# Order of copies, splits, loads and banks in the last third of a decoder layer kernel

## The chip, the cores and the metric

The kernel runs on one core of a Trainium2 chip. The core has a matmul engine (TensorE, PE in the profile; PEld is its weight load, which overlaps with it), a vector engine (VectorE, DVE), an activation engine (ScalarE, ACT), a general engine (GpSimd, POOL) and a queue engine (SyncE, SP) that here only issues transfers. Each runs its own list of instructions in order and waits on semaphores for the others. The metric is the device time of one execution in microseconds (us); the median of several runs counts.

## The reference

One layer on x of 512 tokens by 1024, in float32: three token mixers in parallel (a gated MLP over chunks, sparse attention, a recurrent block), merged through gates and an output projection, then a SwiGLU. Cut to what matters here:

```python
h = rms_norm(x, g_pre_mix)
z = h @ w_in
u, v, q, kv, nsa_g, xr, rg, mg = jnp.split(z, split_points, axis=-1)
...
merged = (gates[:, :, 0] * (y_a @ w_br_a)
          + gates[:, :, 1] * (y_b @ w_br_b)
          + gates[:, :, 2] * (y_c @ w_br_c))
x = x + rms_norm(merged @ w_o, g_post_mix)

hf = rms_norm(x, g_pre_ffn)
f_gate, f_up = jnp.split(hf @ w_ffn_in, 2, axis=-1)
f = (jax.nn.silu(f_gate) * f_up) @ w_ffn_out
return x + rms_norm(f, g_post_ffn)
```

`w_ffn_in` is 1024 by 5632 (gate and up of 2816 each), `w_ffn_out` 2816 by 1024.

## The kernel before

**Numbers.** A float32 operand goes to PE as two parts: `hi`, a copy on ACT rounded to the type that PE multiplies at full rate (line L131 in the profile), and `lo`, the rest, a subtraction on DVE (L136). `split` issues both. A product is then three matmuls: hi by hi, hi by lo, lo by hi.

**Block products.** Where it can, the kernel cuts a matrix product into 2x2 blocks and computes it with seven block products in place of eight, after the scheme of Strassen in Winograd's form: sums and differences of blocks are made on DVE ahead (`s13`, `a21`, `a22` for the weights; `tokens` for the other side), and the seven results are added in PSUM banks or on DVE.

**c stage.** In an earlier part, `b_pair` computes the branch projections with such products while `wload` prepares weight tiles for later; `wload` loads a tile on SP and splits it. `with tc.issue_after(x)` puts what it holds behind instruction x in the scheduler's list, so on each engine behind what stands there by then.

**Gate and up, `ffn_head` and `pairs`.** The 22 column pairs of `w_ffn_in` (a gate tile and the up tile beside it) are computed for two halves of the tokens. `ffn_head` does the first two pairs (`HEAD = 2`) with plain passes for the first half of tokens; `passes` runs over eight blocks k of the depth, from block `turn` on. `pairs` does the other 20 (j = 2 to 21). A pair is seven products `a11, s1, s2, a12, s4, s3, a22`, each of 12 matmuls of 128x256, 84 in all; PE runs them as a11, s1, (a22 of the pair before), s2, a12, s4, s3. The product z of s2 is copied to `r1` on ACT, that of s1 to `r3`, y (a12 and s4) is added to `r1` on DVE, silu follows on ACT; z of s3 is copied to `r2` on ACT, `r3` is added on DVE; after a22 of the pair, `r1 * r2` gives the slab `f`.

**Weights of a pair.** Its raw tile `rawp` holds two rows of tiles per partition, u = 0 (raw0: a11 and a12) and u = 1 (raw1: a21 and a22), 1 MB in all, in one of two alternating buffers (j = 5 has a third). `pair_prep(j)` is a generator in five steps: split raw0 and make `s13` from both halves; split `s13`; split a22 and make a21 in place; make a22 in place; split raw1 (now holding what products s2 and s4 need) and load pair j + 2 into the same buffer (`pair_load`). The split tiles come from a ring of five. `pairs` takes a step of the preparation of pair j + 1 between the products of pair j. What order results on each engine, the scheduler settles from the order of issue and the buffers. The lines are L1698 for the load, L1717 s13, L1726 a21, L1728 a22, L1740 the matmuls, L1768, L1771, L1781 and L1798 the copies of a11, s1, s2 and s3, L1792 the add to r1, L1793 silu, L1799 the add to r2, L1755 the product into f.

**Last projection, `down`.** Seven block products of four quarters q each, 12 matmuls of 128x512 a quarter, with plain `block`s for the part that the scheme leaves over. `fo["prep"]` makes the operands of a quarter: (b) the weights and (a) the tokens, each split by ACT and DVE; for some, `down_add` lets a transfer on POOL's queue add the next weight block into the raw tile after the split. `product(n, q)` runs over two depth blocks i and two PSUM banks m. At the end the last units' blocks are done for each of four token rows c, and `close` finishes row c (L1876 the matmuls of all this).

Of the kernel before, what the change touches and what calls it, by code (L numbers as in the profile page):

```python
# [27 lines left out]
AF = mybir.ActivationFunctionType  # L28
# [24 lines left out]
def hybrid_block(ctx: ExitStack, tc: tile.TileContext, A, out):  # L53
# [84 lines left out]
    res = {}  # L138
# [109 lines left out]
    def unit():  # L248
        i = wcur[0]
        wcur[0] += 1  # L250
        wload(i + 3)
        return wready.pop(i)
# [1064 lines left out]
    def c_stage(first):  # L1317

        c_raw(0)
        gelu = (*res["hid"], res["w1"])  # L1320
        sums = after(gelu, yc_sums())
        second = compress(1)

        def begin():
            for _ in range(4):
                next(sums)
                yield
                head = res["hi"]
            prep = after((head, res["sum"], *gelu), b_prep(0))
            for g in (prep, prep, first, prep, sums, sums, prep, prep, sums, sums, prep):  # L1330
                next(g)
                if g is first:
                    compress_w2(1)
                yield
            c_raw(1)
            c_raw(2)

        run([c_gate(2), hidden(second), c_gate(3)], begin(), 1.5)
        more = seq(second, gmlp_prep(), v_norm())

        def load():
            with tc.issue_after(res["out"].ins):
                wload(wlimit[0])

        for p in range(4):
            pair = b_pair(p, "c")
            third = res["s3"]
            prep = iter(())
            for i, _ in enumerate(pair, 1):
                if p < 3:  # L1350
                    if i == 3:
                        wlimit[0] += 1
                        load()
                    if i == 4:
                        prep = after((*third, res["out"]), b_prep(p + 1))
                    if p and i in (4, 5, 6, 7, 9):
                        next(prep)
                elif i == 2:
                    wlimit[0] = B0 + 4
                    with tc.issue_after(res["out"].ins):  # L1360
                        wload(C0 + 9)
                elif i == 5:
                    with tc.issue_after(res["out"].ins):
                        wload(C0 + 10)
                if i in ((), (1, 2, 3, 5, 7, 8), (), (1, 2, 3, 5, 7, 9))[p]:
                    next(more, None)
            if p == 0:
                wlimit[0] += 1
                load()
                next(prep)  # L1370
            for n, j in enumerate({0: (4, 5), 1: (6,), 2: (7,), 3: ()}[p]):
                if p == 0:
                    next(more)
                side = itertools.islice(more, 3 if p == 1 else 0) if p else itertools.islice(prep, 3 if n == 0 else 1)
                run([c_gate(j)], side, 1.0)
            for _ in prep:
                pass
            if p == 0:
                c_raw(3)
        for _ in more:  # L1380
            pass
# [197 lines left out]
    def ffn_head(n):  # L1579

        us, bs = [], []
        for i in range(2 * n):
            us.append(unit())
            bs.append(bank("mm"))
            yield from passes(bs[i], *us[i], res["fh"], res["fl"], n1=256, turn=0 if i else 4)
            yield

        z, y = ff["zy"] = bank("mm")[:, :256], bank("mm")
        yield from product_parts(z, n, "a11", 11)
        yield from product_parts(y[:, :256], n, "a12", 21)  # L1590

        for j in range(n):
            for k0 in range(0, NK, 4):
                for i in (2 * j, 2 * j + 1):
                    hi, lo = us[i]
                    for k in range(k0, k0 + 4):
                        for t, (w, x) in enumerate(((hi, res["fh"]), (hi, res["fl"]), (lo, res["fh"]))):
                            PE.matmul(bs[i][:, 256:], w[:, k * 128:k * 128 + 128], x[k][:, 256:], start=(k == t == 0),  # L1598
                                      stop=(k == NK - 1 and t == 2))
                        if k % 2:  # L1600
                            yield
            ffn_out(j, bs[2 * j], bs[2 * j + 1])
# [90 lines left out]
    def pair_raw(j):  # L1693
        return ff["raw"][2 if j == HEAD + 3 else (j - HEAD) % 2]

    def pair_load(j):
        if HEAD <= j < NFF:
            SY.dma_start(pair_raw(j), A["w_fi"][2 * j:2 * j + 2].rearrange("u p n -> p u n"))  # L1698

    def pair_prep(j):  # L1700

        if j >= NFF:
            return
        raw = pair_raw(j)
        r4 = raw.rearrange("p u (h n) -> p (u h) n", h=2)
        a11, a12, a21, a22 = (r4[:, i] for i in range(4))
        g = [ff["ring"][(3 * (j - HEAD) + i) % 5] for i in range(3)]
        w = wa[j] = {}

        def halves(u, *names):  # L1710
            for i, n in enumerate(names):
                w[n] = tuple(t[:, 512 * i:512 * i + 512] for t in u)

        split(raw[:, 0], *g[0])
        halves(g[0], "a11", "a12")
        s13 = stage.tile([128, 1024], F32, tag="raw", name=nm("s13"), bufs=2)
        V.tensor_tensor(s13.rearrange("p (i n) -> p i n", i=2), r4[:, 0:4:3], a21[:, None, :].to_broadcast([128, 2, 512]),  # L1717
                        op=OP.subtract)
        yield
        split(s13, *g[1])  # L1720
        halves(g[1], "s3", "s1")
        yield
        side = 32 * ((j - HEAD + 1) % 2)
        w["a22"] = row("a22h", F32R, "tg", side), row("a22l", F32R, "q32", side)
        split(a22, *w["a22"])
        V.tensor_add(a21, s13[:, 512:], a11)  # L1726
        yield
        V.tensor_sub(a22, a12, a21)  # L1728
        yield
        split(raw[:, 1], *g[2])  # L1730
        halves(g[2], "s2", "s4")
        if j != HEAD + 1:
            pair_load(j + 2)
        yield

    def product_parts(ps, j, a, b, start=True):
# [8 lines left out]
    def pairs():  # L1745
# [12 lines left out]
        for j in range(HEAD, NFF):  # L1758
# [31 lines left out]
            yield  # L1790
            product(y[:, 256:], j, "s4", 22, False)
            V.tensor_add(r1, y, r1)  # L1792
            res["silu"] = SC.activation(r1, r1, AF.Silu)  # L1793
            next(prep, None)
            yield
            r2 = row("r2")
            product(z, j, "s3", 3, False)
            SC.activation(r2[:, 256:], z, AF.Copy)  # L1798
            V.tensor_add(r2[:, 256:], r2[:, 256:], r3[:, :256])  # L1799
            wa[j].update(z=z, r1=r1, r2=r2)  # L1800
            next(prep, None)
            yield
        down_begin()
        wlimit[0] = len(wlist)
# [24 lines left out]
    def down_begin():  # L1829
        s1 = slab("fs1", tag="y", shape=(NQ, 2, 256))  # L1830
        for q in range(NQ):
            f = ff["slab", q]
            for i in range(2):
                for h in range(2):
                    fo[f"a{h + 1}{i + 1}", q] = f[:, i:4:2, 256 * h:256 * h + 256]
            fo["s1", q] = s1[:, q]
        fo["n"] = 0
        fo["a"] = {}

        def prep(n, q, hi, lo):  # L1840
            a, b, after = {1: ("a11", "c", (0, 1)), 2: ("a12", "b", None), 5: ("s1", "c", (1, 1)),
                           6: ("a11", "c", (1, 0)), 3: ("a12", "d", (0, 1)), 7: ("a21", "d", None),
                           4: ("a22", "c", None)}[n]
            e = (2, 3, 0, 1)[fo["n"] % 4]
            fo["n"] += 1
            split(fo[b, q], *(t.rearrange("p (i n) -> p i n", i=2) for t in (hi, lo)))
            if after:
                down_add(b, q, *after)
            u = ff["unit"][e // 2][:, e % 2].rearrange("p (l i t) -> p l i t", l=2, i=2)
            fo["a"][n, q] = u[:, 0], u[:, 1]  # L1850
            split(fo[a, q], u[:, 0], u[:, 1])
        fo["prep"] = prep

    def fo_sum(name, q):
# [8 lines left out]
    def down():  # L1863
# [24 lines left out]
        def product(n, q):  # L1888
            ps = {1: z, 6: z, 7: z, 4: z, 2: y, 5: w, 3: w}[n]
            bh, bl = unit()  # L1890
            ah, al = fo["a"].pop((n, q))
            for i in range(2):
                f = slice(512 * i, 512 * i + 512)
                for m in range(2):
                    t = slice(128 * m, 128 * m + 128)
                    mac(ps[m], (ah[:, i, t], bh[:, f]), (ah[:, i, t], bl[:, f]), (al[:, i, t], bh[:, f]))

        def plain(h, i):
# [78 lines left out]
        plain(1, NS + 2)  # L1977
        products(4, *((close, 1, c) for c in range(4)))
        us = [unit() for _ in range(NS, NP)]
        for c in range(4):  # L1980
            for i, u in enumerate(us):
                block(0, c, NS + i, *u)
            close(0, c)


# [217 lines left out]
```

## Time and profile before

| what | value |
|---|---|
| three runs | 1092.98, 1093.83, 1094.03 us, median 1093.83 |
| span of the profiled execution | 1090.5 us |
| the median over that span | 3.3 us more |
| DMA, mean over the span | 106 GB/s |
| split, lo of the gate/up halves and others (L136, lo<-raw) | 104 instructions, 1164 ns each |

The span runs from the first to the last instruction that the profiler saw; a time measured from outside has some us around it, and no other time of the profiled execution itself is on record. On the page the busy share of each engine stands first; the chain of waits names, from the end backwards, what each engine waited for; a timeline row shows start, length, engine, line, what it writes and reads, and in brackets the idle time ahead of it and what ended it. In the names, `mm` and `tr` are PSUM banks, `t` and `fh`, `fl` tokens, `hi`, `lo` and `u` split weights, `r` rows of the pair, `s` the tile s13.

### The profile page before, as it was taken

Reading aid. Unit: us, or ns where it says so; the run is one execution under the profiler, and the core shown is the slowest. Engines: PE = TensorE matmul, PEld = TensorE weight load, DVE = VectorE, ACT = ScalarE, POOL = GpSimd, SP = SyncE. Lnnn points to the kernel's source line nnn. Section 1 sums busy time; section 2 is a strip of 40 time slices with the busy share of each in tenths; the row PEclk is TensorE's granted clock in tenths of the full one; section 3 lists DMA queues with packets and bytes.
Section 4 is the critical chain, followed back from the end, with each engine's and each line's share of the span. In section 5 each row is a group of like instructions: output and inputs, shape, how many; then the busy total and the mean of one; then the engine's idle time right before and its main releaser. Section 6 shows DMA issues by size and latency. Waiting matters only on the chain.

```text
span 1090.5 us, 16726 instructions
## 1 busy us (share of the span) xinstructions
PE 1080.7 (99%) x6440; PEld 948.2 (87%) x6440; DVE 883.2 (81%) x1552; ACT 658.9 (60%) x1207; POOL 30.2 (3%) x43
## 2 busy tenths in 40 slices
PE   9999999999999999999999999999999999999997
PEld 7888888999889888898888789988999999998885
DVE  6967779669675899998998887877987888889665
ACT  6757574454444676876777655555656665667552
POOL 1000000000000000000000000000000000022200
PEclk9999999999999999999999999999999999999999
DMA  8332325420322211102111134261323232379902
GB/s 313 104 103 84 97 85 199 182 99 20 116 78 78 78 59 39 59 20 78 59 39 59 58 119 134 76 251 39 117 78 117 100 117 94 135 213 219 185 21 96
DMA packets 34943, 115.06 MB, mean 106 GB/s; under 512 B 3440, under 2 KB 3728, under 8 KB 33968
## 3 DMA queue, kind: packets, MB, share of 16 engines
q1 hardware_dynamic: 28064, 96.93, 26.0%
q0 software_dynamic: 5216, 11.18, 5.1%
q10 hardware_dynamic: 1584, 5.90, 1.4%
q8 instruction: 50, 0.82, 0.3%
q14 instruction: 29, 0.24, 0.1%
HBM read 111.89 MB, written 2.10 MB: 105 GB/s over the span
## 4 chain that ended last, share of the span: by engine, by line
PE 96%; DVE 2%; DMA 1%; ACT 1%; issue 0%; SPq 0%; DVEq 0%; ACTq 0%
PE mm L259 37%; PE mm L1740 16%; PE mm L1876 7%; PE mm L1260 7%; PE mm L1496 4%; PE o L979 4%; PE mm L614 4%; PE sc L941 3%; PE tr L966 3%; PE tr L1876 3%; PE mm L857 2%; PE tr L771 1%; PE tr L498 1%; PE mm L1598 1%; DMA raw<-in_w_v 1%; PE tr L674 1%
## 5 line engine op out<-in xcount | busy, mean ns | idle before, releaser
L259 PE MATMUL mm<-hh,hi 128*128 128x512 f32 x504 | 199.5, 396 | 0.0
L259 PE MATMUL mm<-hh,lo 128*128 128x512 f32 x504 | 197.4, 392 | 0.0
L259 PE MATMUL mm<-hl,hi 128*128 128x512 f32 x504 | 197.0, 391 | 0.0
L136 DVE TENSOR_TENSOR lo<-raw,hi 128x1024 fp32r<-128x1024 f32 (+1 forms) x104 | 121.1, 1164 | 36.9 <-ACT hi L131 34.0
L131 ACT ACTIVATE hi<-raw 128x1024 fp32r<-128x1024 f32 (+1 forms) x104 | 105.2, 1011 | 50.3 <-PE mm L259 18.9
L259 PEld LDWEIGHTS mm<-hh,lo 128*128 128x128 f32 x504 | 94.6, 188 | 19.6
L259 PEld LDWEIGHTS mm<-hl,hi 128*128 128x128 f32 x504 | 94.7, 188 | 18.4 <-issue 0.2
L259 PEld LDWEIGHTS mm<-hh,hi 128*128 128x128 f32 x504 | 94.7, 188 | 18.1 <-PE mm L1260 0.2
L947 ACT ACTIVATE P<-P,ast 128x128 f32<-128x128 f32 (+3 forms) x128 | 70.7, 555 | 23.0 <-DVE ast L945 22.2
L945 DVE CUSTOM_DVE_ANT_0 P<-sc,mask 128x128 f32<-128x128 f32 (+3 forms) x128 | 57.9, 484 | 8.1 <-PE sc L941 7.3
L131 ACT ACTIVATE ph<-tr 128x512 fp32r<-128x512 f32 x80 | 46.9, 592 | 26.2 <-PE tr L966 23.0
L136 DVE TENSOR_TENSOR pl<-tr,ph 128x512 fp32r<-128x512 f32 x80 | 54.4, 686 | 2.9 <-ACT ph L131 0.9
L941 PE MATMUL sc<-K,q 128*128 128x512 f32 (+2 forms) x192 | 51.0, 368 | 0.0
L1740 PE MATMUL mm<-t,hi 128*128 128x256 f32 x288 | 50.7, 276 | 0.0
L1876 PE MATMUL mm<-hi,u 128*128 128x512 f32 x160 | 50.4, 390 | 0.1
L966 PE MATMUL tr<-ident,P 128*128 128x128 f32 x320 | 48.7, 273 | 0.0
L966 PEld LDWEIGHTS tr<-ident,P 128*128 128x128 f32 x320 | 39.1, 140 | 9.6 <-DVE pl L136 1.0
L136 DVE TENSOR_TENSOR lo<-bs,hi 128x1024 fp32r<-128x1024 f32 x28 | 34.1, 1222 | 13.6 <-ACT hi L131 13.5
L1740 PEld LDWEIGHTS mm<-t,hi 128*128 128x128 f32 x288 | 43.3, 188 | 0.0
L1740 PE MATMUL mm<-fh,hi 128*128 128x256 f32 x144 | 40.0, 278 | 0.0
L1740 PE MATMUL mm<-fh,lo 128*128 128x256 f32 x144 | 39.8, 276 | 0.0
L1740 PE MATMUL mm<-fl,hi 128*128 128x256 f32 x144 | 39.8, 276 | 0.0
(474 smaller groups left out, 2895.0 us busy)
## 6 DMA issues: line engine op xcount, KB each, us to landing
raw<-in_w_in SPq DMA_DIRECT2D x64, 512.0 KB, 3.5
rawp<-in_w_fi SPq DMA_DIRECT2D x20, 1024.0 KB, 4.8
bs<-in_w_fo POOLq DMA_DIRECT2D x20, 512.0 KB, 7.4
raw<-in_w_br SPq DMA_DIRECT2D x14, 512.0 KB, 3.5
w<-in_cw ACTq DMA_DIRECT2D x4, 1024.0 KB, 7.3
raw<-in_w_o SPq DMA_DIRECT2D x8, 512.0 KB, 3.9
bs<-in_w_fo SPq DMA_DIRECT2D x8, 512.0 KB, 7.9
raw<-in_w_v SPq DMA_DIRECT2D x7, 512.0 KB, 5.1
```

The costliest lines, as they stand in the source:

```text
L131: res["hi"] = SC.activation(hi, src, AF.Copy)
L136: res["lo"] = V.tensor_sub(lo, src, f32(hi))
L259: res["mm"] = PE.matmul(ps[:m, n0:n1], w[:, k * 128:k * 128 + m], x[k][:, n0:n1], start=(t == 0), stop=(t == 3 * NK - 1))
L614: res["mm"] = PE.matmul(b[c], x[k][:, c * 128:(c + 1) * 128], w[:, kk * 512:kk * 512 + 512], start=(k == 0 and t == 0), stop=(k == NK - 1 ...
L941: PE.matmul(ps[:, :w * n].rearrange("p (b n) -> p b n", b=w), lhs, K[:, i, brs[0]:brs[-1] + 1, :n], start=(i == 0), stop=(i == 1))
L945: V.tensor_tensor_reduce(out=t, in0=ps[:, b * n:b * n + n], in1=mask[0][:, S - n:], scale=-0.125, scalar=3.0e38, op0=OP.add, op1=OP.min, a ...
L947: SC.activation(t, t, AF.Exp, scale=-1.0, bias=st[:, 0, j, b:b + 1], accum_out=st[:, 1, j, b:b + 1])
L966: PE.transpose(pt[:, j * 128:(j + 1) * 128], self.part(j, br)[:, kt * 128:(kt + 1) * 128], ident)
L979: PE.matmul(po, VV[:, kt, g % 2, br].rearrange("p i d -> p (i d)"), x, start=(br == 0 and kt == 0 and t == 0), stop=(br == 1 and kt == a a ...
L1260: res["mm"] = PE.matmul(ps, u[:, k * 128:k * 128 + 128], v[:, k], start=(start and k == t == 0), stop=(k == 3 and t == 2), skip_group_chec ...
L1740: res["mm"] = PE.matmul(ps, w[:, k * 128:k * 128 + 128], x[:, k], start=(start and k == t == 0), stop=(k == 3 and t == 2), skip_group_chec ...
L1876: PE.matmul(ps, a, b, start=id(ps) not in begun, stop=i == len(ops) - 1, skip_group_check=True)
```

## The change

It touches seven places, all of them orders; sums, products and shapes stay.

1. c stage: in the last `b_pair`, the weight tile `C0 + 9` is loaded and split one step later, behind the copy of another product.
2. `ffn_head`: the first unit runs over depth blocks 0 to 7, no longer 4 to 7 and then 0 to 3.
3. `pair_load` may load one half; in `pair_prep` half 0 of pair j + 2 is loaded after the a22 step, half 1 after the split of raw1. Twenty transfers of 1 MB become forty of 512 KB; the first two and the third buffer's go together still.
4. `pairs`: the copy of s3 is issued first, and silu and all the rest of the preparation behind that copy.
5. `down`, operands: tokens are split ahead of weights.
6. `down`, products: one PSUM bank after the other, no longer in turns.
7. The end: the blocks of the first leftover unit for c = 0 and 1 are issued ahead of all others.

```diff
-                elif i == 2:
+                elif i == 3:
                     wlimit[0] = B0 + 4
                     with tc.issue_after(res["out"].ins):
                         wload(C0 + 9)
...
-            yield from passes(bs[i], *us[i], res["fh"], res["fl"], n1=256, turn=0 if i else 4)
+            yield from passes(bs[i], *us[i], res["fh"], res["fl"], n1=256)
...
-    def pair_load(j):
+    def pair_load(j, *us):
         if HEAD <= j < NFF:
-            SY.dma_start(pair_raw(j), A["w_fi"][2 * j:2 * j + 2].rearrange("u p n -> p u n"))
+            for u in us or (0, 1):
+                SY.dma_start(pair_raw(j)[:, u], A["w_fi"][2 * j + u])
...
         V.tensor_sub(a22, a12, a21)
+        if j != HEAD + 1:
+            pair_load(j + 2, 0)
         yield
         split(raw[:, 1], *g[2])
         halves(g[2], "s2", "s4")
         if j != HEAD + 1:
-            pair_load(j + 2)
+            pair_load(j + 2, 1)
         yield
...
             V.tensor_add(r1, y, r1)
-            res["silu"] = SC.activation(r1, r1, AF.Silu)
-            next(prep, None)
             yield
             r2 = row("r2")
             product(z, j, "s3", 3, False)
-            SC.activation(r2[:, 256:], z, AF.Copy)
+            copied = SC.activation(r2[:, 256:], z, AF.Copy)
             V.tensor_add(r2[:, 256:], r2[:, 256:], r3[:, :256])
             wa[j].update(z=z, r1=r1, r2=r2)
-            next(prep, None)
+            with tc.issue_after(copied.ins):
+                res["silu"] = SC.activation(r1, r1, AF.Silu)
+                for _ in prep:
+                    pass
             yield
...
+            u = ff["unit"][e // 2][:, e % 2].rearrange("p (l i t) -> p l i t", l=2, i=2)
+            fo["a"][n, q] = u[:, 0], u[:, 1]
+            split(fo[a, q], u[:, 0], u[:, 1])
             split(fo[b, q], *(t.rearrange("p (i n) -> p i n", i=2) for t in (hi, lo)))
             if after:
                 down_add(b, q, *after)
-            u = ff["unit"][e // 2][:, e % 2].rearrange("p (l i t) -> p l i t", l=2, i=2)
-            fo["a"][n, q] = u[:, 0], u[:, 1]
-            split(fo[a, q], u[:, 0], u[:, 1])
...
-            for i in range(2):
-                f = slice(512 * i, 512 * i + 512)
-                for m in range(2):
-                    t = slice(128 * m, 128 * m + 128)
+            for m in range(2):
+                t = slice(128 * m, 128 * m + 128)
+                for i in range(2):
+                    f = slice(512 * i, 512 * i + 512)
                     mac(ps[m], (ah[:, i, t], bh[:, f]), (ah[:, i, t], bl[:, f]), (al[:, i, t], bh[:, f]))
...
+        for c in range(2):
+            block(0, c, NS, *us[0])
         for c in range(4):
             for i, u in enumerate(us):
-                block(0, c, NS + i, *u)
+                if i or c > 1:
+                    block(0, c, NS + i, *u)
             close(0, c)
```

How the order of the pairs moves on the engines is seen in three places of the built programs. The first is ACT in the middle of the pairs, from the copy of a11 of a pair on; before, it reads:

```order
L1768 ACTIVATE r_1298_8395<-mm_8393 128x256
L1771 ACTIVATE r_1299_8396<-mm_8394 128x256
L131 ACTIVATE a22h_8456<-rawp_7450 128x512
L1754 ACTIVATE r_1295_8378<-mm_8279 128x256
L1781 ACTIVATE r_1298_8395<-mm_8393 128x256
L131 ACTIVATE u_7423<-rawp_7450 128x1024
L131 ACTIVATE hi_6932<-s_1308_8538 128x1024
L1793 ACTIVATE r_1298_8395<-r_1298_8395 128x512
L1798 ACTIVATE r_1303_8491<-mm_8393 128x256
L131 ACTIVATE hi_6930<-rawp_6846 128x1024
```

Here `u_7423<-rawp_7450` is the split of raw1 of the next pair, `hi_6932<-s` that of s13, `hi_6930<-rawp_6846` that of raw0 of the pair after. The same stretch of ACT in the changed program, from the copy of a11 (now L1771) on, where `u_7424<-rawp_7452` is raw0 and the last row raw1:

```order
L1771 ACTIVATE r_1306_8520<-mm_8518 128x256
L1774 ACTIVATE r_1307_8521<-mm_8519 128x256
L131 ACTIVATE a22h_8581<-rawp_6846 128x512
L1757 ACTIVATE r_1303_8499<-mm_8404 128x256
L1784 ACTIVATE r_1306_8520<-mm_8518 128x256
L131 ACTIVATE u_7425<-s_1316_8664 128x1024
L131 ACTIVATE u_7424<-rawp_7452 128x1024
L1799 ACTIVATE r_1311_8613<-mm_8518 128x256
L1803 ACTIVATE r_1306_8520<-r_1306_8520 128x512
L131 ACTIVATE hi_6935<-rawp_6846 128x1024
```

The split of raw1 went from ahead of s13's split to the end, behind the copy of s3 (L1799) and silu (L1803), which changed places with each other; the split of raw0 went ahead of both. The second place is DVE in the middle of the pairs, from the add to r1 on; before:

```order
L1792 TENSOR_TENSOR r_1298_8395<-mm_8394,r_1298_8395 128x512
L136 TENSOR_TENSOR u_7423<-rawp_7450,u_7423 128x1024
L136 TENSOR_TENSOR lo_6933<-s_1308_8538,hi_6932 128x1024
L1799 TENSOR_TENSOR r_1303_8491<-r_1303_8491,r_1299_8396 128x256
L136 TENSOR_TENSOR lo_6931<-rawp_6846,hi_6930 128x1024
L136 TENSOR_TENSOR a22l_8570<-rawp_6846,a22h_8569 128x512
L1755 TENSOR_TENSOR f_8326<-r_1298_8395,r_1303_8491 128x512
L1728 TENSOR_TENSOR rawp_6846<-rawp_6846 128x512
L1717 TENSOR_TENSOR s_1316_8651<-rawp_7450 128x1024
L1726 TENSOR_TENSOR rawp_7450<-s_1316_8651,rawp_7450 128x512
```

The second row is the lo part of raw1. In the changed program DVE's list there reads as follows, from the s13 step on; the names in brackets are the semaphores that an instruction waits for (DMAHW those of transfers):

```order
L1718 TENSOR_TENSOR s_1283_8207<-rawp_7452 128x1024 [waits DMAHW7_49,DMAHW6_49]
L1727 TENSOR_TENSOR rawp_7452<-s_1283_8207,rawp_7452 128x512 [waits DVE_49]
L1795 TENSOR_TENSOR r_1273_8063<-mm_8062,r_1273_8063 128x512 [waits PE_49,Activation_49]
L136 TENSOR_TENSOR lo_6936<-s_1283_8207,hi_6935 128x1024 [waits Activation_49]
L136 TENSOR_TENSOR lo_6934<-rawp_7452,hi_6933 128x1024 [waits PE_49,Activation_49]
L1800 TENSOR_TENSOR r_1278_8156<-r_1278_8156,r_1274_8064 128x256 [waits Activation_49]
L136 TENSOR_TENSOR lo_6932<-rawp_6846,hi_6931 128x1024 [waits Activation_49]
```

The lo part of raw1 moved from directly behind the add to r1 to behind those of s13 and raw0 and the add to r2 (the last row), and s13 waits for two transfers. The third place is DVE in the first pairs, the end of pair 2; before, the third row is the lo part of raw1 of pair 3:

```order
L1792 TENSOR_TENSOR r_1232_7528<-mm_7357,r_1232_7528 128x512
L136 TENSOR_TENSOR lo_6935<-s_1242_7632,hi_6934 128x1024
L136 TENSOR_TENSOR lo_6931<-rawp_7450,hi_6930 128x1024
L1799 TENSOR_TENSOR r_1237_7585<-r_1237_7585,r_1233_7529 128x256
L136 TENSOR_TENSOR lo_6933<-rawp_6846,hi_6932 128x1024
L1717 TENSOR_TENSOR s_1250_7745<-rawp_7452 128x1024
```

And after, where it is the last row:

```order
L1795 TENSOR_TENSOR r_1232_7532<-mm_7359,r_1232_7532 128x512
L136 TENSOR_TENSOR lo_6936<-s_1242_7636,hi_6935 128x1024
L1718 TENSOR_TENSOR s_1250_7750<-rawp_7455 128x1024
L1800 TENSOR_TENSOR r_1237_7586<-r_1237_7586,r_1233_7533 128x256
L136 TENSOR_TENSOR lo_6934<-rawp_6846,hi_6933 128x1024
L136 TENSOR_TENSOR lo_6932<-rawp_7452,hi_6931 128x1024
```

Three instructions, s13 of pair 5, the add to r2 and the lo part of raw0 of pair 4, now stand ahead of it.

## The prediction

> **What bounds the kernel now.** I read the page's head and busy table first, then the chain of waits, then the timeline of each engine inside the stages that the change touches.
>
> ```profile
> span 1090.5 us, 16726 instructions
> ...
> PE 1080.7 (99%) x6440; PEld 948.2 (87%) x6440; DVE 883.2 (81%) x1552; ACT 658.9 (60%) x1207; POOL 30.2 (3%) x43
> ```
>
> TensorE (PE) is busy for 99% of the span. A reorder that adds no matmul and takes none away can win only what PE loses in the stages it touches. The chain shows those stages, as start, length and count of matmuls:
>
> ```profile
> 250.64 9.57 PE mm L1260 x84
> 265.68 9.89 PE mm L1260 x84
> ...
> 803.25 9.80 PE mm L1740 x84
> 813.06 155.23 PE mm L1740 x1367
> 1037.23 13.60 PE mm L1876 x60
> 1053.55 30.24 PE mm L1876 x132
> ```
>
> 1367 matmuls of 128x256 take 155.23 us, so one takes 0.1136 us and a pair of 84 takes 9.54 us, with no hole in it. 60 matmuls of 128x512 take 13.60, so one takes 0.2267. The losses stand around these pieces, in the PE rows (start, busy time, what, idle time before and its releaser):
>
> ```profile
> 758.33 0.30 PEld L259 LDWEIGHTS mm<-fh,u 128*128 128x128 f32 x2 [0.39 <-ACT fh L131]
> ...
> 802.82 0.28 PE L1740 MATMUL mm<-t,lo 128*128 128x256 f32 x1
> 803.25 0.51 PE L1740 MATMUL mm<-t,a22h 128*128 128x256 f32 x2 [0.15 <-ACT r L1798]
> ...
> 972.77 0.99 PE L1876 MATMUL mm<-hi,u 128*128 128x512 f32 x2
> ...
> 1005.89 0.62 PE L1876 MATMUL tr<-hi,u 128*128 128x512 f32 x2
> 1006.57 0.90 PE L1876 MATMUL tr<-hi,u 128*128 128x512 f32 x2
> ```
>
> **What the change can remove.** The c stage: 9.89 against 9.57, 0.3. The head's first unit: 0.39 of idle weight load; its tokens still come from ACT, so I take half, 0.2. Pair 3: 802.82 to 803.25 where one matmul needs 0.11, less the 0.02 of rounding, 0.3 to 0.4 (0.4). Pair 4: 9.80 against 84 x 0.1136, 0.3. Down's first product: two matmuls in 0.99 against about 0.62 in the same form at 1005.89, 0.4. The copies into s5: 0.90 against 0.62, 0.3. The last blocks: 30.24 against 132 x 0.2267 = 29.92, 0.3. Together **2.2 us**. Each edit could win nothing or its full row: 0 to 2.2. If a later split or bank comes late instead, the nearest row for such a miss is 0.43 (802.82 to 803.25), so down's two edits could also cost up to 0.9.
>
> Costed at nothing: the 20 more load issues on SP, 0.37 each by the row further down, on a queue with nothing else in this stage. The accumulating load of down now stands behind one more split pair per quarter; its rows are read eight products later (96 matmuls of 0.2267, 21.8 us), against a landing of 7.4, so the cover would have to shrink by 14 us. No arithmetic instruction is added.
>
> **What the pair edit adds.** In a steady pair J, the built order on ACT is: split of s13(J+2), split of raw0(J+2), copy of s3(J), silu(J), split of raw1(J+1), r1, r3. So the copy isn't the first thing after s3; the split of raw0 stands before it, and it writes a ring tile that s3(J) reads, so it starts only when s3(J) has ended. And the split of raw1(J+1), whose product s2 runs in pair J+1, stands last; before, it stood ahead of the other two splits. On DVE the times of the same steps, in the old order, are:
>
> ```profile
> 857.31 1.22 DVE L136 TENSOR_TENSOR lo<-rawp,hi 128x1024 fp32r<-128x1024 f32 x1
> 858.45 0.68 DVE L1792 TENSOR_TENSOR r<-mm,r 128x512 f32<-128x512 f32 x1
> 859.05 1.22 DVE L136 TENSOR_TENSOR u<-s,u 128x1024 fp32r<-128x1024 f32 x1
> 860.18 1.22 DVE L136 TENSOR_TENSOR lo<-rawp,hi 128x1024 fp32r<-128x1024 f32 x1
> 861.32 0.42 DVE L1799 TENSOR_TENSOR r<-r,r 128x256 f32<-128x256 f32 x1
> 863.33 1.23 DVE L1717 TENSOR_TENSOR s<-rawp 128x1024 f32<-128x1024 f32 x1 [1.59 <-DMA rawp<-in_w_fi]
> 864.47 0.69 DVE L1755 TENSOR_TENSOR f<-r,r 128x512 f32<-128x512 f32 x1
> ...
> 865.68 0.68 DVE L1726 TENSOR_TENSOR rawp<-s,rawp 128x512 f32<-128x512 f32 x1
> 866.28 0.69 DVE L1728 TENSOR_TENSOR rawp<-rawp 128x512 f32<-128x512 f32 x1
> ```
>
> The first row is lo of raw1. It now comes behind r2 add (861.32 + 0.42), 4.4 us later than before. Instructions overlap a little, so I take start to start: lo of s13 1.13, lo of raw0 1.14, r1 add 0.60, s13 1.14, a21 add 0.60; r2 add 0.42 and lo of raw1 1.22 stand at their lengths, the last because another engine waits for their end. ACT in the same way:
>
> ```profile
> 868.02 1.05 ACT L131 ACTIVATE hi<-s 128x1024 fp32r<-128x1024 f32 x1
> 868.98 0.61 ACT L1793 ACTIVATE r<-r 128x512 f32<-128x512 f32 x1
> 869.49 0.37 ACT L1798 ACTIVATE r<-mm 128x256 f32<-128x256 f32 x1
> 869.75 1.05 ACT L131 ACTIVATE hi<-rawp 128x1024 fp32r<-128x1024 f32 x1
> 870.70 0.37 ACT L1768 ACTIVATE r<-mm 128x256 f32<-128x256 f32 x1
> ...
> 787.97 0.28 PE L1740 MATMUL mm<-fh,hi 128*128 128x256 f32 x1
> 788.17 0.39 ACT L1781 ACTIVATE r<-mm 128x256 f32<-128x256 f32 x1 [0.97 <-PE mm L1740]
> ```
>
> Split 0.96, silu 0.51, copy 0.26, and 0.20 from the start of PE's next matmul to ACT's start behind a product (787.97 to 788.17). **First test**: from s3's end to the end of lo of raw1: 0.20 + 0.96 + 0.26 + 0.51 + 1.05 + 0.03 + 1.22 = 4.23. PE wants that lo after a11, s1, a22 and two hi matmuls of s2: 38 x 0.1136 = 4.32. It just fits, with 0.09 left of what were some 4.5.
>
> **Second test**, through the load. Half raw1 of pair J+3 goes into the buffer that split raw1(J+1) has just read; s13(J+3) on DVE needs both halves; and behind it on DVE stand a21 add, r1 add(J+1), lo of s13, lo of raw0, r2 add and lo of raw1(J+2), which lets the next load go. That is a loop of one turn per pair.
>
> ```profile
> 858.56 0.37 SPq L1698 DMA_DIRECT2D rawp<-in_w_fi  x1
> ...
> raw<-in_w_in SPq DMA_DIRECT2D x64, 512.0 KB, 3.5
> rawp<-in_w_fi SPq DMA_DIRECT2D x20, 1024.0 KB, 4.8
> bs<-in_w_fo POOLq DMA_DIRECT2D x20, 512.0 KB, 7.4
> ...
> raw<-in_w_o SPq DMA_DIRECT2D x8, 512.0 KB, 3.9
> ```
>
> The issue follows the split by 0.03 (857.31 + 1.22 = 858.53) and s13 follows the 4.8 of the landing at once. A half is 512 KB in the same form as the x64 row, which takes 3.5. The loop: 0.03 + 3.5 + 1.14 + 0.60 + 0.60 + 1.13 + 1.14 + 0.42 + 1.22 = **9.78 us**, against 9.54 that PE needs. It is 0.24 short, and PE would wait for lo of raw1 in every pair. By ACT in place of DVE (0.03 + 3.5 + 1.23, then the five ACT steps, 0.03 and 1.22) it comes to nearly the same. It is turned once for each s13 of pairs 8 to 21, 14 times: 14 x 0.24 = 3.4, say 3.5 us with what restarts cost.
>
> The landing decides. On the same queue, in a window in which only such loads run:
>
> ```profile
> DMA to landing us min/median/max: 3.3/3.5/3.6
> ```
>
> 3.3 gives 9.58, 14 x 0.04 = 0.6; 3.6 gives 9.88, 4.8; the 3.9 of the w_o loads gives 10.18, 9.0; a half that takes as long as the whole, 4.8, gives 21. The break-even is 3.26. I take 3.5: same size, queue and shape, and the half before it is issued long earlier.
>
> The Trainium skill, page "DMA: Bandwidth & Descriptors", section "Anatomy of one DMA — SWDGE (gpsimd) path", gives a transfer as about 2.0 us and its bytes at 436 GB/s, thus an estimate of 3.2 for 512 KB and 4.4 for 1 MB. The trace shows 3.5 and 4.8, so I stay with the rows; by the page's 3.2 the loop would be 9.48 and would not bind.
>
> **Start-up.** The order of the first pairs differs, and SP's first loads too.
>
> ```profile
> 794.77 0.39 PE L1740 MATMUL mm<-t,hi 128*128 128x256 f32 x2
> ...
> 790.97 0.69 DVE L1792 TENSOR_TENSOR r<-mm,r 128x512 f32<-128x512 f32 x1
> 791.57 1.22 DVE L136 TENSOR_TENSOR lo<-s,hi 128x1024 fp32r<-128x1024 f32 x1
> 792.70 1.22 DVE L136 TENSOR_TENSOR lo<-rawp,hi 128x1024 fp32r<-128x1024 f32 x1
> ```
>
> The row at 792.70 is lo of raw1(3), done at 793.9, with s2's matmuls at 794.77. In the new order s13(5), r2 add and lo of raw0(4) stand between: 791.57 + 1.13 + 1.14 + 0.42 + 1.14 + 1.22 = 796.6. PE, with three matmuls of a12 put ahead in its new order, wants it at 794.77 + 5 x 0.1136 = 795.34. A wait of 1.3, with 0.1 for the restart **1.4**. Pair 4 then starts at about 801.6 and pair 5 at 811.2; lo of raw1(4) ends 4.23 into pair 4, at 805.9; then a load (3.53), s13(6), s13(7), r1 add, lo of s13, r2 add, lo of raw0, lo of raw1(5): 805.9 + 3.53 + 1.14 + 1.14 + 0.60 + 1.13 + 0.42 + 1.14 + 1.22 = 816.2, wanted at 811.2 + 4.32 = 815.5. Another 0.7, with the restart about **0.9**. These two waits could be 0 (if DVE's neighbours come earlier than I have them) or up to 3.
>
> **Sum**, against the profiled span: 1.4 + 0.9 + 3.5 - 2.2 = +3.6, from 1090.5 to 1094.1. The median of the three runs shown is 1093.83, 3.3 above the span, so 1097.5 us.
>
> **Rivals.**
>
> *The loop doesn't bind.* If the halves land in 3.25 or less, the loop is no longer than PE's 9.54, the steady pairs stay closed and only the start-up remains, there smaller too (some 0.6 for the second): 1.4 + 0.6 - 2.2 = -0.2, 1093.6. For it: a minimum of 3.3 in the row and the page's estimate. Against it: the median of 3.5. Chance 0.2, with the 3.3 case up to 1096.
>
> *No new wait at all.* If DVE and ACT hold their deadlines throughout, the 2.2 come in full: 1091.6. Against it stands the 0.09 of the first test. Chance 0.08. The skill's page "Perfetto Trace Analysis", section "DMA Optimizations", holds that smaller pieces let some transfers start sooner, which is this way out; the row of 1.59 idle on DVE shows that there was such a wait to shorten.
>
> *The halves disturb each other.* If the half of raw0, sent in the same pair, takes from that of raw1, the landing is that of the w_o row, 3.9, or more: 9.0 in the loop, 1103; at 4.8, 1115. It decides from about 3.7 upward (6.2 in the loop). Against it: raw0's load starts behind the a22 sub, at least two DVE steps before the other is due. Chance 0.12.
>
> *It doesn't do what it says.* The copy of s3 stands behind the raw0 split, so pair 3's and pair 4's 0.7 may stay, and down's gains may not come: up to +1.6 on the forecast, 1099, inside its range.
>
> **How the numbers follow.** The forecast, loop and start-up waits with landings of 3.35 to 3.7, has 0.6 and spans 1095 to 1101. Two in ten may lie outside the range; I let go the full gain and the upper part of the disturbed case, and set it from 1094.3 to 1101.5. A measurement of this kernel can tell about 0.2%, 2.2 us, from no change. Faster than 1091.6 needs the full gain, 0.08. Within it, to 1096.0, falls the loop that doesn't bind and the low end of the forecast, 0.22. Slower holds the rest, 0.70.
>
> **What would show it.** In the changed kernel's profile: the half loads of rawp landing at 3.5; DVE's s13 (now L1718) idle before it for about 1 us per pair on the DMA; PE idle in L1743 for about 0.24 in each of some 14 pairs, released by DVE's lo, and pairs 9.8 apart; a single wait of 1.4 near 795 and one near 815; and the seven losses above gone. It is wrong if PE's pairs still take 9.54 each: then lo of raw1 is not late, and I have an instruction's place or the landing wrong. It is wrong the other way if PE waits for another tile, above all for the raw0 split, or in down for tokens.

## Result and profile after

| | median us | lowest to highest | span of the profiled run |
|---|---|---|---|
| before | 1093.63 (4 runs) | 1092.98 to 1094.03 | 1090.5 |
| changed | 1103.75 (4 runs) | 1102.70 to 1104.75 | 1101.5 |

The ratio is 1.0094 with a 95% interval of 1.0080 to 1.0109: slower by 10.1 us, where 3.6 were forecast, and outside the range (1094.3 to 1101.5 us). The way was right, the size was not.

From the page of the changed kernel, its head, two groups of section 5 and the loads of the pairs in section 6:

```profile
span 1101.5 us, 16798 instructions
...
L1743 PE MATMUL mm<-t,lo 128*128 128x256 f32 x144 | 41.1, 285 | 3.2 <-DVE lo L136 3.1
L1718 DVE TENSOR_TENSOR s<-rawp 128x1024 f32<-128x1024 f32 x20 | 24.4, 1224 | 23.4 <-DMA rawp<-in_w_fi 23.4
...
rawp<-in_w_fi SPq DMA_DIRECT2D x40, 512.0 KB, 3.6
```

PE is still busy 99% by the page, and this group of its matmuls waited only 3.2 us in all: the page hardly shows the loss on PE. By the starts of PE's matmuls in the pairs, 8.9 us lie in gaps between them and 3.6 us in stretches of a slower pace (last section); before, these were 0.7 and less than 0.1. On DVE the loss shows as 23.4 us of waits, in s13, for loads. Next, the chain of waits inside 812 to 840 and 840 to 900 us, the middle of the pairs (start, length, what):

```profile
825.06 4.88 DMA rawp<-in_w_fi
```

```profile
839.98 1.24 DVE s L1718
841.25 0.04 DVE rawp L1727
841.28 0.57 issue
841.86 0.60 DVE r L1795
842.46 2.35 DVE lo L136 x2
844.80 0.34 DVE r L1800
845.14 1.20 DVE lo L136
846.36 3.42 DMA rawp<-in_w_fi
...
849.88 1.24 DVE s L1718
...
856.25 4.59 DMA rawp<-in_w_fi
...
860.94 1.24 DVE s L1718
...
880.80 1.24 DVE s L1718
...
887.17 4.99 DMA rawp<-in_w_fi
...
892.26 1.23 DVE s L1718
```

Before, this chain was one piece of 1367 matmuls. Now it is the forecast loop, step by step: s13, a21 add (L1727, with 0.04 us and 0.57 of "issue" behind it), r1 add, lo of s13, lo of raw0, r2 add, lo of raw1, load, s13. A plain turn, 839.98 to 849.88, takes 9.90. But two turns here are long: 849.88 to 860.94 is 11.06 and 880.80 to 892.26 is 11.46, and the load in them landed after 4.59 and 4.99, not 3.42. The load of 825.06, before these, took 4.88.

PE is no part of this loop. In each of the 14 turns DVE's rows from the start of s13 to the end of lo of raw1 take 6.34 to 6.35 us without idle time, and then comes the load. At 867 the view goes through PE for 5.4 us to an r1 add, but this add too starts 1.87 us behind s13, as in every turn. PE's slower pace doesn't set the turn either: behind 867.56, 82 matmuls came 113 ns apart, PE then waited for lo of raw1, and the turn (870.89 to 880.80) was 9.91 all the same.

The stages that the change touches outside the pairs, in the chain: before, the head's first piece

```profile
758.38 10.85 PE mm L259 x90
...
774.53 0.57 PE mm L1598 x5
```

and after, the head, the c stage's last product and the last blocks:

```profile
265.93 9.57 PE mm L1260 x84
...
758.28 10.21 PE mm L259 x90
773.86 1.25 PE mm L1598 x11
...
1007.47 24.51 PE tr L1880 x108
...
1048.29 13.60 PE mm L1880 x60
1064.61 29.93 PE mm L1880 x132
```

The c stage's piece lost its 0.32 (9.89 to 9.57), the head 0.64 (10.85 to 10.21), the last blocks 0.31 (30.24 to 29.93), and the copies into s5 no longer break the piece of 108. From the head's L1598 to the piece of 60 before the last blocks it took 1037.23 - 774.53 = 262.7 before, and 1048.29 - 773.86 = 274.4 after: nearly 12 us more, all in the pairs.

### The profile page after: what moved, and what is told of

The parts are those of the page before. It is cut to its first block, busy times and chain, and to the rows that moved or that the text cites. A ratio compares the mean times of both kernels' runs of the same rounds, so it can differ in the third digit from the quotient of the medians.

```text
span 1101.5 us, 16798 instructions
## 1 busy us (share of the span) xinstructions
PE 1088.6 (99%) x6440; PEld 953.7 (87%) x6440; DVE 884.7 (80%) x1552; ACT 655.7 (60%) x1207; POOL 30.3 (3%) x43
## 4 chain that ended last, share of the span: by engine, by line
PE 86%; DVE 8%; DMA 4%; issue 1%; ACT 1%; SPq 0%; DVEq 0%
PE mm L259 37%; PE mm L1880 7%; PE mm L1260 7%; PE mm L1743 6%; PE mm L1496 4%; PE mm L614 4%; PE o L979 4%; PE sc L941 3%; DMA rawp<-in_w_fi 3%; PE tr L966 3%; DVE lo L136 3%; PE tr L1880 3%; PE mm L857 2%; DVE u L136 2%; PE tr L771 1%; DVE s L1718 1%
## 5 line engine op out<-in xcount | busy, mean ns | idle before, releaser
L1743 PE MATMUL mm<-t,lo 128*128 128x256 f32 x144 | 41.1, 285 | 3.2 <-DVE lo L136 3.1
L1718 DVE TENSOR_TENSOR s<-rawp 128x1024 f32<-128x1024 f32 x20 | 24.4, 1224 | 23.4 <-DMA rawp<-in_w_fi 23.4
```

The lines of the kernel that those rows point to most:

```text
L1743: res["mm"] = PE.matmul(ps, w[:, k * 128:k * 128 + 128], x[:, k], start=(start and k == t == 0), stop=(k == 3 and t == 2), skip_group_chec ...
```

## Experiments

Two theories of the twelve microseconds. **The loop**: each turn from one split of raw1 through the load to the next is longer than PE's 9.54. **The place**: the split of raw1, behind copy and silu, comes too late from the end of the products before it, whatever the load. Besides, a cause of the long turns is sought.

**1. Both edits of the pairs undone.** The pairs' code is that of before; the other five edits stay.

```diff
-                SY.dma_start(pair_raw(j)[:, u], A["w_fi"][2 * j + u])
+            SY.dma_start(pair_raw(j), A["w_fi"][2 * j:2 * j + 2].rearrange("u p n -> p u n"))
...
-            with tc.issue_after(copied.ins):
-                res["silu"] = SC.activation(r1, r1, AF.Silu)
-                for _ in prep:
-                    pass
```

> The changed kernel with both edits of the pairs undone (whole loads, old order of copy, silu and the last split); the c stage, the head and the last projection stay changed. If the pairs carry the loss, the pairs stage goes back to its old length and only the small gains stay: 1092 to 1093, faster than before by 1 to 1.5 us. If the other edits cost something too, it stays above 1094.

Measured 1092.11 us against 1093.69 of the kernel before, ratio 0.9981 (0.9970 to 0.9992). The whole loss is in the two edits of the pairs, and the rest of the change wins about 1.6 us. It is the fastest kernel of this study, though by a difference close to what can be told.

**2. Old order, loads by halves; 3. the same with only silu behind the copy.**

> The loads by halves stay, the order of copy, silu and the last split is the old one. Theory of the loop (the split of raw1 frees the buffer, the half is loaded, s13 and the splits behind it on the vector engine lead to the next split of raw1): the splits of s13 and raw0 and the add to r2 no longer stand ahead of the split of raw1, the turn is 2.7 us shorter, about 7.2 us, far below 9.54: no wait, 1092 to 1093. Rival, that halves disturb each other or cost by themselves: above 1096.

> As the changed kernel, with the copy of s3 ahead of silu, but the last step of the preparation (split of raw1 and its load) taken where the old order takes it, ahead of the copy. Theory of the loop: no wait, 1091.5 to 1093. Rival, that silu behind the copy is what costs: as the changed kernel, 1103.

Measured 1097.51 (ratio 1.0033, 1.0020 to 1.0046) and 1095.71 (1.0020, 1.0012 to 1.0028). Both theories missed: the steady turn of the vector engine is not too long, yet the kernel loses. In the first of them PE waits here, in a product a22, for the copy of s3 (the row's releaser), and ACT's rows show what stood ahead of that copy; the waits view sums it up for the weight load:

```profile
941.59 0.50 PE L1743 MATMUL mm<-t,a22h 128*128 128x256 f32 x2 [0.94 <-ACT r L1801]
```

```profile
937.62 1.06 ACT L131 ACTIVATE hi<-rawp 128x1024 fp32r<-128x1024 f32 x1 [3.35 <-DVE rawp L1729]
938.59 1.04 ACT L131 ACTIVATE hi<-s 128x1024 fp32r<-128x1024 f32 x1
939.53 1.04 ACT L131 ACTIVATE hi<-rawp 128x1024 fp32r<-128x1024 f32 x1
940.63 0.63 ACT L1796 ACTIVATE r<-r 128x512 f32<-128x512 f32 x1
941.17 0.36 ACT L1801 ACTIVATE r<-mm 128x256 f32<-128x256 f32 x1
```

```profile
PEld mm L1743 <- ACT r L1801: 4.8, 11, 1.2
```

Three splits, for pairs ahead, run back to back before silu and the copy, because the first had to wait for a22 sub on DVE. By DVE's rows s13, which waits for its load, stands ahead of that a22 sub in nearly every pair with halves, and only in every second with whole loads. Why the scheduler chose so isn't shown; presumably it expects the halves earlier. So an edit of the loads alone moves instructions on ACT and DVE, and PE's gaps, nearly all ahead of a22 and for that copy, came with that order; the second of the two runs has nine such waits, 4.0 us in all.

**4. New order, whole loads.**

> The new order stays, the loads are whole again (4.8 us to landing, not 3.5). The scheduler then puts the split of s13 behind that of raw1 on the vector engine. Theory of the loop, by its built order: 4.83 load, 1.26 s13, 0.60 a21 add, 1.14 lo of raw0, 0.38 r2 add, 1.22 lo of raw1 = 9.43 us, just below 9.54: pairs nearly closed, 1092 to 1095, faster than by halves though each load is longer. Rival, that the split of raw1 behind copy and silu is too late by itself, whatever the load: 1103. Rival, that only the landing counts and the order on the vector engine doesn't: 9.95 plus 1.3 per turn, over 1115.

Measured 1099.79 (1.0052, 1.0038 to 1.0066): faster than the halves, as the loop says and both rivals deny, but 5 us above the number given. From 836 to 855 us its chain shows PE, and then a load:

```profile
836.11 13.98 PE mm L1740 x118
...
855.44 6.24 DMA rawp<-in_w_fi
```

118 matmuls in one piece: here the plain turn leaves PE nearly closed (s13 follows s13 by 9.5 to 9.9 us). But a long load (6.24, with 5.0 as this kernel's median) has no slack to fall into, as the turn was forecast only 0.1 below PE's: the two turns with loads of over 6 us took 10.9 and 11.0.

**5 and 6. The same 0.6 us of vector work, inside the loop and outside it.**

```diff
+        V.tensor_add(a21, s13[:, 512:], a11)
         V.tensor_add(a21, s13[:, 512:], a11)
```
```diff
+        V.tensor_sub(a22, a12, a21)
         V.tensor_sub(a22, a12, a21)
```

> The changed kernel with the in-place add to a21 done twice (the second gives the same values). On the vector engine it stands between s13 and the split of raw1, so inside the loop from one split of raw1 through the load to the next. Theory of the loop: 0.60 us more in each of 14 turns, 8.4 us: about 1112, turns of 10.55. Rival, that the split of raw1 is late only by its place behind copy and silu on the scalar engine: no more than 1 us, since the vector engine has 1.4 to 2.4 us idle in each pair.

> The changed kernel with the subtraction to a22 done twice (the second gives the same values): the same 0.60 us of vector work per pair, but where it waits for the load, between the split of raw1 and s13, so outside the loop. Theory of the loop: hidden, 1103 to 1105. Rival, that the vector engine has too much work in a pair: as much as for a21, about 1112.

Measured 1109.86 (1.0153, 1.0135 to 1.0170) and 1102.21 (1.0082, 1.0064 to 1.0100). Inside the loop it cost 7.7 us more than outside it, and outside it nothing beside the changed kernel. The waits of s13 for loads fit (total, times, longest), first of the kernel with the work inside, then of that with the work outside:

```profile
DVE s L1718 <- DMA rawp<-in_w_fi: 27.4, 15, 3.2
```
```profile
DVE s L1718 <- DMA rawp<-in_w_fi: 10.6, 15, 1.7
```

Outside, the work was done in the time in which DVE waits anyway (23.4 in the changed kernel). As with experiment 4, the theory of the place can't explain this.

**7. Raw0 loaded behind raw1.**

```diff
-        if j != HEAD + 1:
-            pair_load(j + 2, 0)
...
-            pair_load(j + 2, 1)
+            pair_load(j + 2, 1, 0)
```

> The changed kernel with both halves of a pair loaded behind the split of raw1, raw1 first and raw0 right behind it. The order on the engines is that of the changed kernel, but s13 waits for 1 MB in place of 512 KB, 4.8 to 5.2 us. Theory of the loop: turns of 11.3 to 11.6 us, 14 times 1.4 to 1.7 more: 1121 to 1127. Rival, that the place of the split counts and not the load: 1103.

Measured 1102.60 (1.0083, 1.0067 to 1.0099). It tells nothing of the theories: the built lists of DVE, ACT and SP read as in the changed kernel in the pairs, row for row, since the scheduler issues the load of raw0 when its buffer is free, wherever the code asks for it. It is a second copy of the changed kernel. One turn of its trace took over 11 us, not two in the same stretch.

**8. 32 instructions fewer on PE.** For the long turns: the transfers inside two windows of the changed kernel, one with a long landing (856 to 861 us) and one with a plain one (846 to 850), by queue, with packets, MB and the share of 16 engines:

```profile
q1 hardware_dynamic: 212, 0.80, 56.7%
q8 instruction: 1, 0.02, 1.3%
```
```profile
q1 hardware_dynamic: 152, 0.56, 48.9%
```

One 16 KB piece on the instruction queue lies in the first. The page has 50 of them in 0.82 MB; PE runs 6440 matmuls and as many weight loads, so 50 pieces are about one for each 256 of its instructions. The edit shifts them against the pairs:

```diff
-    for _ in range(11):
+    for _ in range(3):
         PE.matmul(pw[:, :128], ones, ones, start=True, stop=True)
```

> The changed kernel with 3 in place of 11 warm-up matmuls at the very start, 32 instructions fewer on the matmul engine. The trace of the changed kernel shows a 16 KB transfer on the instruction queue every 256 of that engine's instructions, and the loads of raw1 that it falls into take 4.4 to 5.0 us to land, not 3.5. With 32 instructions fewer it comes about 1.9 us later in each pair, when the load of raw1 has mostly landed. Theory of the fetch: none or one of the turns over 10.5 us left, the pairs some 3 to 4 us shorter, the whole 1099.5 to 1101 (the start may cost or gain up to 1 us by itself, so the pairs count). Rival, that the long turns come from the pattern of the buffers: turns unchanged, every third one over 11 us.

Measured 1102.55 (1.0082, 1.0066 to 1.0098), no less than the changed kernel again (experiment 10), so the time forecast was missed. The waits of s13 fell from 23.4 to:

```profile
DVE s L1718 <- DMA rawp<-in_w_fi: 18.9, 15, 2.2
```

The turns up to 929 us took 9.8 to 10.0 each; the long ones at 830, 861 and 892 are gone, and two of 10.7 and 10.3 came at the end of the pairs. In the pairs that is 2 to 3 us less, the start took back about one. But in this trace the pieces still begin inside the loads of those three turns, 2.8 to 3.2 us behind their issue, so they didn't leave the loads, as had been expected. Over the seven traces with this order and half loads, the packets' times say more. Of the landings of raw1, all 16 of 4.5 us or more (4.5 to 5.05) have a piece that began 1.0 to 3.0 us behind the issue. The 65 without a piece took 3.25 to 3.84. All six with a piece that began within 1.0 to 1.8 us are long; of those at 2.7 to 3.2 some are, and 16 aren't. So the long landings go with a fetched piece; that the piece itself holds up the load is the reading that fits, and isn't shown by itself.

**9. A third buffer for raw1.** From pair 6 on raw1 has three tiles; s13 stays in one tile.

```diff
-        s13 = stage.tile([128, 1024], F32, tag="raw", name=nm("s13"), bufs=2)
...
+            s13 = ff["s13"]
+            V.tensor_sub(s13[:, :512], a11, a21)
+            V.tensor_sub(s13[:, 512:], a22, a21)
...
-            pair_load(j + 2, 1)
+            pair_load(j + 3, 1)
```

> The changed kernel with three buffers for raw1 in place of two, from pair 6 on (the third takes a tile of another pool; s13 then stays in one tile and is made by two subtractions, 0.06 us more). The half of raw1 of a pair is loaded a whole pair earlier; the order of the splits, the copy and silu on the scalar engine is that of the changed kernel. Theory of the loop: it now spans two pairs and doesn't bind; s13 no longer waits for a load, and pairs take 9.54 to 9.65: 1092 to 1094 (the wait of 1.3 in the first pairs stays). Rival, that the split of raw1 is late by its place behind copy and silu: turns still over 9.8 and 1099 or more.

Measured 1103.72 (1.0092, 1.0077 to 1.0108): the theory as stated missed by 10 us, and the rival seemed to hold. The chain of this kernel (900 to 914 us) says why:

```profile
900.04 3.65 DMA rawp<-in_w_fi
...
903.81 0.69 DVE s L1733
...
904.84 2.27 DVE u L136 x2
...
909.67 0.70 DVE rawp L1744
...
910.39 3.50 DMA rawp<-in_w_fi
```

It is a loop through a load again, of 10.35 us in this turn, now that of raw0: the subtraction a22 (L1744) frees raw0, its half is loaded, and the first half of s13 (L1733), which waits for it, had been moved ahead of both splits. With the raw1 loop cut, the scheduler's new order made another one.

**10. The changed kernel once more.**

> The changed kernel once more, for its own spread: 1102 to 1105. If the long turns come from the moment at which an instruction fetch falls into a load, they may stand at other places or be missing in this execution; if they come from the buffers, every third turn is over 11 us as before.

Measured 1102.39 (1.0081, 1.0064 to 1.0098), 1102.07 to 1104.45. In its profiled execution, the slowest of the four, two turns took 11.5 us, in the same stretch as in the first. So they recur in the same program, and not always alike (experiment 7 had one).

**11. A shorter load, in the same order.** The turn of the loop is cut without a new order (but for a few rows of the first pairs), by loading less; so part of the weights is left out of the result:

```diff
-                SY.dma_start(pair_raw(j)[:, u], A["w_fi"][2 * j + u])
+                n = 256 if u and j > HEAD + 3 else 1024
+                SY.dma_start(pair_raw(j)[:, u, :n], A["w_fi"][2 * j + u][:, :n])
```

> The changed kernel, but from pair 6 on only the first 256 of 1024 columns of each raw1 tile are loaded (128 KB in place of 512 KB; the rest of the tile keeps old weights, so part of the weights is left out of the result). The order on the vector engine in the pairs is row for row that of the changed kernel. Theory of the loop: each turn loses what the landing loses, over 0.5 us, so it is shorter than 9.54 and doesn't bind; s13 waits little, turns 9.54 to 9.65: 1093.5 to 1095.5. Rival after the run with a third buffer, that the chain from a product's end through the scalar engine's splits to the split of raw1 sets the turn whatever the load: turns 9.9 and more, 1099 to 1104.

Measured 1095.74 (1.0023, 1.0014 to 1.0032), 7 to 8 us faster than the changed kernel. A quarter of the half mostly lands in 2.0 to 2.1 us:

```profile
rawp<-in_w_fi SPq DMA_DIRECT2D x1, 128.0 KB, 2.1
```

and the wait of s13 is gone but for one (in the waits of DVE):

```profile
DVE s L1719 <- DMA rawp<-in_w_fi: 1.1, 1, 1.1
```

From 905 us on its turns are 9.51 to 9.53, PE's own. The one wait is for a load of 128 KB that took 3.56 us, with a 16 KB piece in it. Over experiment 1, 3.6 us are left: PE's rows give 1.9 for the two waits of the start-up and 0.6 for two later ones, and slower stretches about 1.9 (experiment 1 has 0.6 of waits there itself). This settles the loop: only the load was made shorter, and the turns closed.

**12. The split of raw1 ahead of silu.**

```diff
             with tc.issue_after(copied.ins):
-                res["silu"] = SC.activation(r1, r1, AF.Silu)
                 for _ in prep:
                     pass
+                res["silu"] = SC.activation(r1, r1, AF.Silu)
```

> The changed kernel with the split of raw1 ahead of silu on the scalar engine, not behind it; nothing else moves in the pairs on any other engine, but for one row. Theory of the loop through the vector engine: the split's lo part doesn't wait for its hi part, so turns stay at 9.9 to 10.0: 1101 to 1104. Rival, that the scalar engine's chain sets the turn: 0.51 us less in each, 1096 to 1097.

Measured 1100.58 (1.0059, 1.0042 to 1.0076), between the two. The plain turns stay at 9.8 to 10.0, and s13 waits for loads 21.2 us in all, so the steady loop didn't move, as the theory says. Of what it gained, about 1.4 us lie in the start-up, where the first wait of PE falls from 1.25 to 0.44 and the second, 0.54, is gone; the expectation had left that out.

**13. Whole loads, with only the copy ahead of silu.**

> Whole loads and the old place of the split of raw1, with the copy of s3 ahead of silu, and the c stage, head and last projection as changed. The copy no longer stands behind silu, so the two waits for it near 802 and 812 (0.4 and 0.3 us) go: 1091 to 1092, against 1092.1 without this edit. Rival, as with loads by halves: the splits of s13 and raw0 come ahead of the copy and the products a22 wait for it, 1094 or more.

Measured 1092.72 (0.9987, 0.9977 to 0.9998), no better than 1092.11 without it. The wait at 802 went, but a22 waits at other places (1.2 us near 811, 0.6 near 908): the splits now stand ahead of the copy there. Moving the copy forward isn't worth anything by itself in this kernel.

## Why the prediction was wrong

- **What bounds the kernel**: right. Of the 2.2 us of PE's losses 1.5 lay outside the pairs, and about that was won (experiment 1). The head gave more than forecast (0.6 for 0.2); of the last projection's 1.0 the first product's 0.4 was not won: three matmuls of 0.23 each still take 1.21 there.

```profile
984.18 1.21 PE L1880 MATMUL mm<-hi,u 128*128 128x512 f32 x3
```

- **The first test**, ACT's chain just fits: right. With the load out of the way the turns closed in that very order (experiment 11), and 0.51 us less in the chain changed no plain turn (12).
- **The second test**, the loop through the load: the mechanism was right, its terms stood in the chain in the forecast order, and shortening or lengthening it moved the time (5, 11). The step that failed is the size of "14 x 0.24 = 3.4, say 3.5 us".
  - The plain turn was put at 9.78 and is 9.95: from 892.26 to the last s13 at 961.94 are seven turns, 69.7 us. The load with its hand-over takes 3.6 in the mean, where I had 3.53, and the vector engine's part 6.35, where I had 6.25: a21 add waits for the end of s13 (1.26 from start to start, not 1.14). 14 times 0.17 is 2.4 us. Near a threshold small errors count in full: 0.24 over PE's 9.54 became 0.41.
  - The landing was taken as one number ("I take 3.5"), the median of two groups. Three of the fourteen loads took 4.6 to 5.0, together 4 us more than 3.5 each, in turns of up to 11.5. Before, s13 waited for its load too, 1.6 us in the row shown, and PE's pairs stayed closed; in a loop that binds, each late load counts in full (1.1 and 1.5 us late made turns of 11.06 and 11.46 out of 9.9).
  - These two make up 6.4 of the 6.5 us that the forecast was short of by the medians; by the spans of the two profiled runs it was short of 7.4, so about 1 us stays with the other terms.
- **Start-up**: 1.4 and 0.9 were forecast. PE's rows give 1.36 for the first (794.55 to 795.91, less the 0.11 of the matmul itself, and 0.11 of restart) and 0.65 for the second, near 815.

```profile
794.55 0.28 PE L1743 MATMUL mm<-fh,u 128*128 128x256 f32 x1
795.91 0.39 PE L1743 MATMUL mm<-t,lo 128*128 128x256 f32 x1 [1.08 <-DVE lo L136]
```

- **The rivals**: "the halves disturb each other" had 1103 and 0.12, and the time came out there, but not by its mechanism. The prediction looked at the raw0 of the same pair, sent 7 to 8 us ahead; that of the next pair is sent 1.8 to 2.6 us behind raw1's load in every turn, and the plain ones of raw1 still land in 3.4 to 3.7. Its price was right for a reason that it didn't name. That the range left out its upper part was the mistake: a loop that binds multiplies each error of the landing by 14, and the row of 3.9 for the same size stood on the page. "The loop doesn't bind" and "No new wait at all" fell with the turns of 9.9.
- The Trainium skill's page "DMA: Bandwidth & Descriptors" has, in "Queues, rings and completion order", each of the 16 engines take turns between the queues that it has work for, a packet at a time. The piece on q8 is 1.3% of 16 engines in 5 us, about 1.0 us of one engine, and the loads of the long turns take 1.1 to 1.5 more. This fits the page's rule in its size, and no run shows that it is the same engine.

## What to carry to other kernels

Where a buffer is reloaded after its last reader, write down the loop: reader, load, everything that stands in order ahead of the next reader. Compare it with the bound engine's period, and take the slow loads, not the median, when the two are within a few per cent. Cutting a load in two shortens it, but here the scheduler then moved other work (experiment 2); read the built order of every engine before costing such an edit. The same work put in twice, once where it costs nothing and once where it costs over half a microsecond a turn (experiments 5 and 6), is a cheap way to find out what is in the loop.

## What the runs showed of the hardware

PE's matmuls of 128x256 came at two paces, and the slower one has its own stretches. In the run with the short load, two windows of 5 us, the first behind the wait near 794 (window, length, PE's busy time and count, clock, share of DMA, GB/s; matmuls that a window cuts are counted too):

```profile
795.70:800.70 5.00, 5.00 (x44) 1.00 0.40 123
806.00:811.00 5.00, 5.00 (x46) 1.00 0.08 25
```

By their starts the matmuls came 118 ns apart for some 65 of them, then 113 ns as before, at a granted clock of 1.00 in both. That is 0.3 us for a stretch, which the page doesn't show as idle. Many such stretches begin behind a wait, but it is no rule: in the same run three of some 70 matmuls begin without one (834.55, 892.82, 950.37), and in the changed kernel the matmuls behind the waits near 867, 928 and 958 kept 113 ns. In the pairs of the changed kernel 859 of 1664 matmuls came at the slower pace, before the change 6. What causes it wasn't tried.
